# Turning the second unit of each weight-stationary sum, and a smaller bias-row store on another queue

## The chip, the cores and the metric

The kernel runs on one core of one Trainium2 chip. The metric is the time of one execution on the device in microseconds (us), without the host's part. Three runs of the kernel before took 2806.85, 2808.48 and 2808.56 us; the median is 2808.48 us. A profiled execution is one further run, with its own time and its own span (from the first instruction to the last).

## What is computed

A two-layer decoder trunk on one sequence of 256 tokens with model width 2048, all in float32. Layer 0 mixes tokens by retention (8 heads), layer 1 by attention (16 heads of 128) on keys and values that come from the stream after layer 0; each layer then has a squared-ReLU MLP with hidden width 8192 and a gated embedding. Attention adds a bias that depends on the distance between query and key alone:

```python
for i in range(DEPTH):
    if i < N_A_LAYERS:
        h = h + retention(rms_norm(h, ret_norm_g[i]), ret_w_in[i], ret_w_out[i])
    else:
        h = h + moba_attention(rms_norm(h, att_norm_g[j]), att_w_q[j], att_w_o[j],
                               k_blocks, v_blocks, k_means, rel_bias)
    h = h + sq_relu_mlp(rms_norm(h, mlp_norm_g[i]), mlp_w_up[i], mlp_w_down[i])
    h = h + per_layer_embed(h, p[i], ple_norm_g[i], ple_w_up[i], ple_w_gate[i])
return rms_norm(h, final_norm_g)
# inside the attention, with one block of 256 keys:
l_own = jnp.where(dist_own[None] >= 0, l_own + bias_t[:, t5_bucket(dist_own)], NEG_INF)
```

Nearly all the work is the products of the 256 token columns with some 500 MB of weights, each weight used once.

## The kernel before

**Units.** All weights are cut into units of 128 x 1024 numbers (512 KB). Two units come in one load of 1 MB, named `raw` (line 96), issued on the sync engine's queue (SP). `split` (lines 221 and 222) makes two tiles of each unit: `wh`, the weights rounded to the matmul's short format, by a cast on the scalar engine (ACT), and `wl`, what the rounding left, by a subtraction on the vector engine (DVE). Activations are split in the same way into a high part (columns 0 to 255 of a tile) and a low part (columns 256 to 511).

**The sum.** In `mm_a` the weights are the stationary operand. A unit is 8 blocks of 128 rows. First come 8 matmuls with the blocks of `wh` on all 512 columns (line 160; high times high and high times low), then 8 with the blocks of `wl` on the 256 high columns (line 162; low times high). I call them wide and narrow here. `phase_a` runs a weight matrix so: an output tile of 128 rows (`n`) needs `per` units (`u`), 2 or 4 of them, all summed in one PSUM bank. The first `lead` tiles are interleaved (all their units `u` = 0, then all their `u` = 1, and so on), the later ones come one after the other. Phases of this kind have the tile names `qk`, `ret_out`, `up`, `dn`, `gt`, `ak`, `aq` and `att_o`, 788 such units in all. The values and gates of the heads (`v`, `g`, `av`) go through `phase_b` instead, where the activations are stationary and every matmul is wide (lines 212 to 214); `pu` (lines 566 to 568) has narrow ones alone.

**The order of the work** is written out by hand. `run` goes through the units: at unit `i` it issues the load of units `i + 6` and `i + 7` (`load`, for even `i`), the split of unit `i + 3` (`conv`), the matmuls of unit `i`, and then the tasks that `at(i, ...)` hung on that unit, such as the evacuation of a finished bank. Each engine takes its instructions in this order. There are 3 `raw` buffers, 4 of `wh` and 4 of `wl`; a load waits for the subtraction that last read its buffer, a cast waits for the matmuls that last read its `wh`.

**The bias.** `bias_rows` makes 16 rows of 384 numbers, one for each head (`bv`, a small matmul at line 611 and a copy at line 613), while the last units of layer 0's MLP run (`dn`). Line 616 stores them to a scratch tensor `bvec` in HBM, each row 128 times, from SP's queue. In the attention, `table` loads for each group of 4 heads two tiles `T` of 128 x 2 x 256 (line 642): partition p reads copy p of a row, shifted by p, which gives the bias for every query and key.

Of the kernel before, what the change touches and what calls it, by code (L numbers as in the profile page):

```python
# [10 lines left out]
F32 = mybir.dt.float32  # L11
# [6 lines left out]
P = 128  # L18
S = 256
# [5 lines left out]
AH, DH = 16, 128  # L25
GH = 4
# [7 lines left out]
LEAD = 4  # L34
LOOK = 3
WARM = 8
G_RET, G_MLP0, G_PLE0, G_KV, G_ATT, G_MLP1, G_PLE1, G_FIN = range(8)


def order_a(tiles, per, lead):  # L40
    out = [(n, u) for u in range(per) for n in range(lead)]
    return out + [(n, u) for n in range(lead, tiles) for u in range(per)]
# [31 lines left out]
class Core:  # L74
# [70 lines left out]
        return self.wp.tile([P, S], F32, name=name, tag="small", bufs=6)  # L145


    def mm_a(self, ps, wh, wl, rhs, first, last, narrow=False):
        mm = self.nc.tensor.matmul
        cut = [slice(k * P, (k + 1) * P) for k in range(8)]  # L150
        if narrow:
            o = ps[:, :S]
            for k, c in enumerate(cut):
                x = rhs[k]
                mm(o, wh[:, c], x[:, :S], start=first and k == 0, stop=False)
                mm(o, wh[:, c], x[:, S:], start=False, stop=False)
                mm(o, wl[:, c], x[:, :S], start=False, stop=last and k == 7)
            return
        for k, c in enumerate(cut):
            mm(ps, wh[:, c], rhs[k], start=first and k == 0, stop=False)  # L160
        for k, c in enumerate(cut):
            mm(ps[:, S:], wl[:, c], rhs[k][:, :S], start=False, stop=last and k == 7)  # L162

    def phase_a(self, name, src, base, tiles, per, lead, rhs, evac, narrow=(), rush=()):


        banks, ends = {}, {}
        for j, (n, u) in enumerate(order_a(tiles, per, lead)):
            def mm(wh, wl, n=n, u=u):
                if u == 0:  # L170
                    banks[n] = self.bank(f"{name}{n}")
                self.mm_a(banks[n], wh, wl, [rhs(u * 8 + k) for k in range(8)], u == 0, u == per - 1, n in narrow)
            i = self.unit(src, base + j, mm)
            if u == per - 1:
                ends[n] = i
                self.at(i, lambda n=n, i=i: self.steps(i, evac(n, banks.pop(n)), 4 if n in rush else 2 if n == tiles - 1 else 1))
        return ends
# [115 lines left out]
    def start(self):  # L293
# [4 lines left out]
        nc.scalar.activation(warm, self.ones, AF.Silu)  # L298
        self.warm(WARM)
        self.hh = [cp.tile([P, 4, S], F32, name=f"h{q}") for q in range(4)]  # L300
# [297 lines left out]
    def bias_rows(self, i):  # L598
        nc, cp, io = self.nc, self.cp, self.io
        st = {}  # L600

        def load():
            st["rb"] = cp.tile([33, AH], F32, name="relb")
            nc.vector.memset(st["rb"][32:33], NEG)
            nc.sync.dma_start(st["rb"][:32], io["rel_bias"])
            st["oh"] = self.slot("oh", (33, 384))
            nc.sync.dma_start(st["oh"], io["onehot"])

        def rows():
            ps = self.aux("bv")  # L610
            nc.tensor.matmul(ps[:AH, :384], st["rb"], st["oh"], start=True, stop=True)
            st["bv"] = self.slot("bv", (AH, 384))
            nc.vector.tensor_copy(st["bv"], ps[:AH, :384])

        def store():
            nc.sync.dma_start(io["bvec"], st["bv"][:, None, :].to_broadcast([AH, P, 384]))
        self.at(i, load)
        self.at(i + 6, rows)
        self.at(i + 8, store)

    def attention(self):
        nc = self.nc
        mm = nc.tensor.matmul
        first = len(self.units)
# [8 lines left out]
        for g in range(AH // GH):  # L633
            b, st = len(self.units), {}

            def table(st=st, g=g):
                st["T"] = []
                bv = self.io["bvec"]
                for j in range(0, GH, 2):
                    t = self.slot("T", (P, 2, S))  # L640
                    src = bass.AP(tensor=bv.tensor, offset=bv.offset + (g * GH + j) * P * 384 + 127, ap=[[383, P], [P * 384, 2], [1, S]])
                    nc.sync.dma_start(t, src)
                    st["T"] += [t[:, 0], t[:, 1]]
            self.at(b, table)

            def evac_k(n, ps, st=st):
# [91 lines left out]
def program(nc, io):  # L738
    with tile.TileContext(nc) as tc, tc.manual_schedule(), \
            tc.tile_pool(name="const", bufs=1) as cp, tc.tile_pool(name="w", bufs=1) as wp, \  # L740
            tc.tile_pool(name="slots", bufs=59) as sp, \
            tc.tile_pool(name="psum", bufs=1, space=bass.MemoryType.PSUM) as pp, \
            tc.tile_pool(name="dram", bufs=1, space=bass.MemoryType.DRAM) as dp:
        io["bvec"] = dp.tile([AH, P, 384], F32, name="bvec")
        c = Core(nc, tc, (cp, wp, sp, pp), io)
        c.at(-1, c.start)
        c.retention()
        c.x2 = {}
        c.mlp(0, [G_PLE0])
        c.bias_rows(len(c.units) - 30)  # L750
        c.ple(0, [G_KV, G_ATT])
        c.attention()
        c.mlp(1, [G_PLE1])
        c.ple(1, [G_FIN])
        c.end()
        c.run()
# [62 lines left out]
```

## Time and profile before

| What | Value |
|---|---|
| median of three runs | 2808.48 us |
| the profiled execution | 2807.01 us, span 2805.2 us |
| TensorE matmuls (PE) | 2772.9 us busy, 99% of the span, 15482 matmuls |
| TensorE weight loads (PEld) | 2422.7 us, 86% |
| VectorE (DVE) | 1803.8 us, 64% |
| ScalarE (ACT) | 1346.6 us, 48% |
| weights and other DMA | 521.95 MB, mean 186 GB/s |

In the rows that follow, a time at the start of a row is us from the start of the span; the second is the duration of a run of equal instructions, "x8" their count. What stands in square brackets is the time that the engine sat idle before, and what ended it. A matmul's end is modelled and overlaps the next one, so the pace of TensorE is read from the distance between starts. Rows of SP and SPq are issues of transfers; how long a transfer took to land is in the view of DMA issues.

### The profile page before, as it was taken

Reading aid. Unit: us, or ns where it says so; the run is one execution under the profiler, and the core shown is the slowest. Engines: PE = TensorE matmul, PEld = TensorE weight load, DVE = VectorE, ACT = ScalarE, POOL = GpSimd, SP = SyncE. Lnnn points to the kernel's source line nnn. Section 1 sums busy time; section 2 is a strip of 40 time slices with the busy share of each in tenths; the row PEclk is TensorE's granted clock in tenths of the full one; section 3 lists DMA queues with packets and bytes.
Section 4 is the critical chain, followed back from the end, with each engine's and each line's share of the span. In section 5 each row is a group of like instructions: output and inputs, shape, how many; then the busy total and the mean of one; then the engine's idle time right before and its main releaser. Section 6 shows DMA issues by size and latency. Waiting matters only on the chain.

```text
span 2805.2 us, 37950 instructions
## 1 busy us (share of the span) xinstructions
PE 2772.9 (99%) x15482; PEld 2422.7 (86%) x15482; DVE 1803.8 (64%) x2633; ACT 1346.6 (48%) x1901; POOL 0.2 (0%) x4
## 2 busy tenths in 40 slices
PE   9999999999999999999979999999999999999997
PEld 7888888888888888888869888888888888888887
DVE  7766666655566555665647876667665556666666
ACT  5444444444455434444436655555454434544454
POOL 0000000000000000000000000000000000000000
PEclk9999999999999999999989999999999999999999
DMA  6455555555555555555574555455555555555553
GB/s 239 177 183 183 183 183 183 183 195 194 182 188 188 190 189 191 182 194 182 195 189 175 200 179 185 173 180 180 189 186 195 180 194 183 194 191 185 196 180 123
DMA packets 78667, 521.95 MB, mean 186 GB/s; under 512 B 8443, under 2 KB 14492, under 8 KB 16796
## 3 DMA queue, kind: packets, MB, share of 16 engines
q1 hardware_dynamic: 78492, 519.52, 52.6%
q8 instruction: 121, 1.98, 0.3%
q14 instruction: 54, 0.44, 0.1%
HBM read 514.25 MB, written 5.24 MB: 185 GB/s over the span
## 4 chain that ended last, share of the span: by engine, by line
PE 98%; DMA 1%; DVE 0%; ACT 0%; SPq 0%; issue 0%; DVEq 0%; ACTq 0%
PE up L160 17%; PE dn L160 16%; PE up L162 9%; PE dn L162 8%; PE ret_out L160 4%; PE gt L160 4%; PE qk L160 4%; PE ret_out L162 2%; PE ak L160 2%; PE att_o L160 2%; PE aq L160 2%; PE v L212 2%; PE v L213 2%; PE v L214 2%; PE g L212 2%; PE g L214 2%
## 5 line engine op out<-in xcount | busy, mean ns | idle before, releaser
L222 DVE TENSOR_TENSOR wl<-raw,wh 128x1024 fp32r<-128x1024 f32 (+1 forms) x970 | 1179.9, 1221 | 450.3 <-ACT wh L221 433.6
L221 ACT CAST wh<-raw 128x1024 fp32r<-128x1024 f32 (+1 forms) x970 | 1013.9, 1048 | 567.9 <-PE dn L160 234.9
L160 PE MATMUL dn<-a,wh 128*128 128x512 f32 x2048 | 514.8, 393 | 14.5 <-ACT wh L221 14.5
L160 PE MATMUL up<-x,wh 128*128 128x512 f32 x2048 | 513.2, 392 | 0.0
L160 PEld LDWEIGHTS dn<-a,wh 128*128 128x128 f32 x2048 | 369.6, 190 | 81.5 <-ACT wh L221 14.7
L160 PEld LDWEIGHTS up<-x,wh 128*128 128x128 f32 x2048 | 368.3, 189 | 65.9
L162 PEld LDWEIGHTS dn<-a,wl 128*128 128x128 f32 x2048 | 280.2, 191 | 20.1
L162 PEld LDWEIGHTS up<-x,wl 128*128 128x128 f32 x2048 | 279.4, 190 | 20.0
L162 PE MATMUL dn<-a,wl 128*128 128x256 f32 x2048 | 286.4, 283 | 0.0
L162 PE MATMUL up<-x,wl 128*128 128x256 f32 x2048 | 285.5, 282 | 0.0
L226 ACT COPY t<-up 128x256 f32<-128x256 f32 x128 | 47.7, 373 | 329.4 <-PE up L162 329.4
L227 DVE TENSOR_TENSOR t<-t,up 128x256 f32<-128x256 f32 x128 | 53.9, 421 | 215.2 <-ACT t L226 215.1
L160 PE MATMUL ret_out<-ot,wh 128*128 128x512 f32 x512 | 128.3, 392 | 0.0
L160 PE MATMUL gt<-x,wh 128*128 128x512 f32 x480 | 120.6, 393 | 0.0
L160 PE MATMUL qk<-x,wh 128*128 128x512 f32 x448 | 112.6, 393 | 0.0
L160 PEld LDWEIGHTS ret_out<-ot,wh 128*128 128x128 f32 x512 | 92.1, 189 | 16.5
L212 PE MATMUL v<-wh,x 128*128 128x512 f32 x256 | 100.4, 392 | 0.0
L213 PE MATMUL v<-wl,x 128*128 128x512 f32 x256 | 99.7, 389 | 0.0
L212 PE MATMUL g<-wh,x 128*128 128x512 f32 x256 | 99.6, 389 | 0.0
L214 PE MATMUL v<-wh,x 128*128 128x512 f32 x256 | 99.6, 389 | 0.0
L160 PEld LDWEIGHTS gt<-x,wh 128*128 128x128 f32 x480 | 86.3, 189 | 15.4
L213 PE MATMUL g<-wl,x 128*128 128x512 f32 x256 | 99.6, 389 | 0.0
(311 smaller groups left out, 3029.9 us busy)
## 6 DMA issues: line engine op xcount, KB each, us to landing
raw<-mlp_up SPq DMA_DIRECT2D x128, 1024.0 KB, 4.9
raw<-mlp_dn SPq DMA_DIRECT2D x128, 1024.0 KB, 4.9
raw<-ret_in SPq DMA_DIRECT2D x94, 1024.0 KB, 4.9
raw<-att SPq DMA_DIRECT2D x48, 1024.0 KB, 4.9
raw<-ret_out SPq DMA_DIRECT2D x32, 1024.0 KB, 4.9
raw<-ple_gate SPq DMA_DIRECT2D x32, 1024.0 KB, 4.9
raw<-att_o SPq DMA_DIRECT2D x16, 1024.0 KB, 4.9
raw<-ple_up SPq DMA_DIRECT2D x4, 1024.0 KB, 4.9
```

Of the source, the lines that this page charges most:

```text
L160: mm(ps, wh[:, c], rhs[k], start=first and k == 0, stop=False)
L162: mm(ps[:, S:], wl[:, c], rhs[k][:, :S], start=False, stop=last and k == 7)
L212: mm_(banks[t], x[:, a], wh[:, c], start=k == 0, stop=False)
L213: mm_(banks[t], x[:, a], wl[:, c], start=False, stop=False)
L214: mm_(banks[t], x[:, b], wh[:, c], start=False, stop=k == KD - 1)
L221: self.nc.scalar.copy(dst_h, src)
L222: self.nc.vector.tensor_sub(dst_l, src, dst_h.bitcast(F32))
L226: self.nc.scalar.copy(dst, ps[:, :S])
L227: self.nc.vector.tensor_add(dst, dst, ps[:, S:])
```

## The change

There are two edits. In `mm_a`, a unit with odd `u` is "turned": its 8 narrow matmuls with `wl` come first and its 8 wide ones with `wh` last. Units with even `u` and the one tile that goes the `narrow` way (the last of `gt`) stay. The same products are summed in the same bank. Secondly, the scratch tensor has 32 copies of each row instead of 128, its store is issued on ACT's queue, and each `T` tile is loaded by four transfers of 32 partitions, where copy p modulo 32 is read at a shift of its own.

```diff
+BR = 32
-        for k, c in enumerate(cut):
-            mm(ps, wh[:, c], rhs[k], start=first and k == 0, stop=False)
-        for k, c in enumerate(cut):
-            mm(ps[:, S:], wl[:, c], rhs[k][:, :S], start=False, stop=last and k == 7)
+        for low in (True, False) if turned else (False, True):
+            for k, c in enumerate(cut):
+                end = last and k == 7 and low != turned
+                if low:
+                    mm(ps[:, S:], wl[:, c], rhs[k][:, :S], start=False, stop=end)
+                else:
+                    mm(ps, wh[:, c], rhs[k], start=first and k == 0, stop=end)
...
-                self.mm_a(banks[n], wh, wl, [rhs(u * 8 + k) for k in range(8)], u == 0, u == per - 1, n in narrow)
+                self.mm_a(banks[n], wh, wl, [rhs(u * 8 + k) for k in range(8)], u == 0, u == per - 1, n in narrow, u % 2 == 1)
...
-            nc.sync.dma_start(io["bvec"], st["bv"][:, None, :].to_broadcast([AH, P, 384]))
+            nc.scalar.dma_start(io["bvec"], st["bv"][:, None, :].to_broadcast([AH, BR, 384]))
...
-                    src = bass.AP(tensor=bv.tensor, offset=bv.offset + (g * GH + j) * P * 384 + 127, ap=[[383, P], [P * 384, 2], [1, S]])
-                    nc.sync.dma_start(t, src)
+                    for q in range(0, P, BR):
+                        src = bass.AP(tensor=bv.tensor, offset=bv.offset + (g * GH + j) * BR * 384 + 127 - q, ap=[[383, BR], [BR * 384, 2], [1, S]])
+                        nc.sync.dma_start(t[q:q + BR], src)
...
-        io["bvec"] = dp.tile([AH, P, 384], F32, name="bvec")
+        io["bvec"] = dp.tile([AH, BR, 384], F32, name="bvec")
```

The first place is TensorE's order at the seam between the two units of one tile of `up` before the change (`wh` and `wl` with their buffer numbers, `x` is the activation, L160 wide, L162 narrow):

```order
L162 MATMUL up_9_6793<-x_6_5484,wl_6711 128x256
L162 MATMUL up_9_6793<-x_7_5577,wl_6711 128x256
L160 MATMUL up_9_6793<-x_8_5670,wh_6738 128x512
L160 MATMUL up_9_6793<-x_9_5763,wh_6738 128x512
L160 MATMUL up_9_6793<-x_10_5856,wh_6738 128x512
L160 MATMUL up_9_6793<-x_11_5949,wh_6738 128x512
```

And the same seam in the changed kernel, where line 165 is the narrow matmul and line 167 the wide one:

```order
L165 MATMUL up_9_6793<-x_6_5484,wl_6711 128x256
L165 MATMUL up_9_6793<-x_7_5577,wl_6711 128x256
L165 MATMUL up_9_6793<-x_8_5670,wl_6739 128x256
L165 MATMUL up_9_6793<-x_9_5763,wl_6739 128x256
L165 MATMUL up_9_6793<-x_10_5856,wl_6739 128x256
L165 MATMUL up_9_6793<-x_11_5949,wl_6739 128x256
```

Narrow now follows narrow at this seam, and at the end of the turned unit wide follows wide. Over the whole program a wide matmul comes right behind a narrow one 518 times instead of 828, and a narrow one right behind a wide one 516 times instead of 860.

The second place is SP's queue at the end of layer 0's MLP, before the change, with the store of the bias rows among the weight loads:

```order
L96 DMA raw_11992<-mlp_dn 128x2048
L96 DMA raw_12045<-mlp_dn 128x2048
L616 DMA bvec<-bv 2048x1x384
L96 DMA raw_12093<-mlp_dn 128x2048
L96 DMA raw_12142<-mlp_dn 128x2048
L96 DMA raw_12189<-mlp_dn 128x2048
```

In the changed kernel the loads follow each other there (line 97 is the load), and the store, 512 rows of 384 now, stands in ACT's order between the casts of `wh_12047` and `wh_12068`:

```order
L97 DMA raw_11992<-mlp_dn 128x2048
L97 DMA raw_12045<-mlp_dn 128x2048
L97 DMA raw_12093<-mlp_dn 128x2048
L97 DMA raw_12142<-mlp_dn 128x2048
L97 DMA raw_12189<-mlp_dn 128x2048
```

The third place is SP's queue at the first group of the attention, before the change:

```order
L96 DMA raw_13613<-att 128x2048
L96 DMA raw_13686<-att 128x2048
L642 DMA T<-bvec 128x2x256 x2
L96 DMA raw_13755<-att 128x2048
L96 DMA raw_13819<-att 128x2048
```

And in the changed kernel, with the four transfers for each `T` tile:

```order
L97 DMA raw_13613<-att 128x2048
L97 DMA raw_13686<-att 128x2048
L648 DMA T<-bvec 32x2x256 x8
L97 DMA raw_13761<-att 128x2048
L97 DMA raw_13825<-att 128x2048
```

Eight issues stand ahead of the next weight load instead of two, in each of the four groups. The program has 8 counters for the completion of transfers, used in turn, so the eighth of these issues also waits for the landing of the load ahead of the first (`raw_13686`), and the load behind them for the landing of the first `T` transfer.

More of the change, by code (lines that the diff above doesn't have):

```diff
@@ L145, in small, with mm_a @@
         return self.wp.tile([P, S], F32, name=name, tag="small", bufs=6)
-    def mm_a(self, ps, wh, wl, rhs, first, last, narrow=False):
+    def mm_a(self, ps, wh, wl, rhs, first, last, narrow=False, turned=False):
         mm = self.nc.tensor.matmul
```

## The prediction

> **What bounds the kernel now.** I read the page first, then the waits of TensorE (PE), then the time lines at the one long wait, then the pace of TensorE in quiet stretches. From the page, busy time by engine, busy tenths in 40 slices, and the chain of work that ended last:
>
> ```profile
> PE 2772.9 (99%) x15482; PEld 2422.7 (86%) x15482; DVE 1803.8 (64%) x2633; ACT 1346.6 (48%) x1901; POOL 0.2 (0%) x4
> PE   9999999999999999999979999999999999999997
> PE 98%; DMA 1%; DVE 0%; ACT 0%; SPq 0%; issue 0%; DVEq 0%; ACTq 0%
> ```
>
> TensorE is the bound nearly everywhere. One slice dips, the 21st (1402 to 1472 us), and the chain has 1% of DMA. Who waited for whom gives the place; first the longest waits of TensorE, then the one of ScalarE behind it:
>
> ```profile
> PE dn L160 <- ACT wh L221: 14.5, 1, 14.5
> PE st L272 <- DVE acc L251: 2.8, 1, 2.8
> ACT wh L221 <- DMA raw<-mlp_dn: 24.4, 1, 24.4
> ```
>
> So there is one wait of 14.5 us, for a cast that waited 24.4 us for a weight load. All else together is a few us. The time lines of SP, ACT and TensorE around it, and the transfers by issue:
>
> ```profile
> 1404.45 0.69 SPq L616 DMA_DIRECT2D bvec<-bv  x1
> 1408.30 47.03 SPq L96 DMA_DIRECT2D raw<-mlp_dn  x6
> ```
> ```profile
> 1396.64 1.05 ACT L221 CAST wh<-raw 128x1024 fp32r<-128x1024 f32 x1 [1.73 <-PE dn L160]
> ...
> 1408.76 1.05 ACT L221 CAST wh<-raw 128x1024 fp32r<-128x1024 f32 x1 [1.74 <-PE dn L160]
> ...
> 1442.61 1.04 ACT L221 CAST wh<-raw 128x1024 fp32r<-128x1024 f32 x1 [24.41 <-DMA raw<-mlp_dn]
> ```
> ```profile
> 1426.22 2.00 PE L160 MATMUL dn<-a,wh 128*128 128x512 f32 x8
> 1428.07 1.11 PE L162 MATMUL dn<-a,wl 128*128 128x256 f32 x8
> 1443.71 3.78 PE L160 MATMUL dn<-a,wh 128*128 128x512 f32 x8 [14.53 <-ACT wh L221]
> 1447.29 1.91 PE L162 MATMUL dn<-a,wl 128*128 128x256 f32 x8
> 1448.99 2.12 PE L160 MATMUL dn<-a,wh 128*128 128x512 f32 x8
> 1450.95 1.11 PE L162 MATMUL dn<-a,wl 128*128 128x256 f32 x8
> 1451.90 2.00 PE L160 MATMUL dn<-a,wh 128*128 128x512 f32 x8
> ```
> ```profile
> bvec<-bv SPq DMA_DIRECT2D x1, 3072.0 KB, 35.1
> raw<-mlp_dn SPq DMA_DIRECT2D x128, 1024.0 KB, 4.9
> T<-bvec SPq DMA_DIRECT2D x8, 256.0 KB, 5.5
> ```
>
> The store of the bias rows is issued at 1404.45 and lands 35.1 us later, at 1439.6. The load issued behind it at 1408.30 lets its cast begin at 1442.61, although such a load lands in 4.9 us elsewhere. The load stood behind the store in the same queue. When TensorE resumes at 1443.71, its first unit runs at half pace (3.78 and 1.91 where 2.00 and 1.11 are usual).
>
> **The bias store: what goes away.** The pace of a unit comes from a quiet stretch of `up`, first and last rows:
>
> ```profile
> 1112.43 2.00 PE L160 MATMUL up<-x,wh 128*128 128x512 f32 x8
> 1114.27 1.12 PE L162 MATMUL up<-x,wl 128*128 128x256 f32 x8
> 1115.22 2.00 PE L160 MATMUL up<-x,wh 128*128 128x512 f32 x8
> ...
> 1274.44 1.78 PE L160 MATMUL up<-x,wh 128*128 128x512 f32 x7
> ```
>
> From 1112.43 to 1274.44 there are 58 units, so a unit takes 162.01 / 58 = 2.793 us. Between 1426.22 and 1451.90 three units were done in 25.68 us, where 3 x 2.793 = 8.38 would do. The store costs 17.3 us: the wait of 14.5 and 2.8 of slow pace behind it.
>
> Does all of it go? The new store has a quarter of the bytes and of the rows, so I scale its landing to 35.1 / 4 = 8.8 us (an estimate). It is on another queue, but take the bad case that the load still lands only after all of the store: 8.8 + 4.9 = 13.7 us after 1408.30, at 1422.0. TensorE would want the unit at 1426.22 + 2.79 = 1429.0, and in the stalled case it began 1.1 us after the cast's start, so a cast at 1427.9 is early enough: 5.9 us to spare. In the good case, sharing the engines, the load lands sooner still. So the whole 17.3 us go. What is late next at that place is the usual order, cast after matmul, as at 1396.64 and 1408.76 (released by PE).
>
> On ACT the store's issue is new. SP took 0.69 us for four times as many rows; the cast behind it, at 1408.76, had sat idle 1.74 us, so up to 0.69 us there is hidden. It waits for the copy of `bv`, two units earlier in the order, as SP did; behind it are only casts with several us of slack (below). Bounds: 0, or 35.1 us of landing if the quarter-size store is no quicker, which is a rival.
>
> **The `T` loads.** SP issues 8 instead of 2 per group. The first group, SP and then ACT:
>
> ```profile
> 1580.62 5.92 SPq L96 DMA_DIRECT2D raw<-att  x2
> 1586.59 0.94 SPq L642 DMA_DIRECT2D T<-bvec  x2
> 1591.11 5.66 SPq L96 DMA_DIRECT2D raw<-att  x2
> ```
> ```profile
> 1602.28 1.05 ACT L221 CAST wh<-raw 128x1024 fp32r<-128x1024 f32 x1
> ```
>
> Two issues took 0.94, so eight take 3.8 us, to 1590.4; the next load began at 1591.11 anyway. The eighth also waits for the load ahead (issued at the end of the 5.92, about 1586.2) to land, at 1591.1, and the next load for the first `T` transfer, 5.5 us after 1586.6, at 1592.1. That makes the load about 1 us late. It lands at about 1597, and its cast, which came at 1602.28 for reasons of TensorE's, doesn't notice: 5 us to spare. Cost 0; without that cover at most 4 x 1 us.
>
> **The turned units: the pace.** The trace shows what a change between wide and narrow costs. Steady wide matmuls are in a value and gate phase (112 starts from the first to the last row), steady narrow ones in `pu` (86 starts):
>
> ```profile
> 124.83 0.39 PE L213 MATMUL v<-wl,x 128*128 128x512 f32 x1
> ...
> 149.99 0.39 PE L213 MATMUL g<-wl,x 128*128 128x512 f32 x1
> ```
> ```profile
> 1485.78 0.28 PE L566 MATMUL pu<-ph,wh 128*128 128x256 f32 x1
> ...
> 1495.98 0.28 PE L567 MATMUL pu<-pl,wh 128*128 128x256 f32 x1
> ```
>
> A steady wide matmul takes 25.16 / 111 = 0.2267 us, a steady narrow one 10.20 / 85 = 0.1200 us. Eight and eight would be 1.813 + 0.960 = 2.773 us, and a unit takes 2.793: 0.020 us more. By the rows of `up`, the wide block takes 1.84 (1112.43 to 1114.27), 0.027 over steady, and the narrow block 0.953 (the rest of 2.793), 0.007 under. So going from narrow to wide costs about 27 ns and going from wide to narrow gives about 7 back. The turned order has 828 - 518 = 310 fewer of the first and 860 - 516 = 344 fewer of the second: 310 x 0.027 - 344 x 0.007 = 8.4 - 2.4 = 6.0 us saved. With the net 0.020 per pair instead, 6.2 to 6.9. The block's 1.84 is rounded to 0.01, which is worth up to 3 us either way on 310 changes if the narrow side doesn't make up for it. I take 6.0, with 4 to 7 as its bounds.
>
> That it is the change of width, and not the start of a unit with fresh weights, I take from the same rows: the stretch from 124.83 to 149.99 holds some nine unit starts (12 wide matmuls each), all with fresh `wh` and `wl`, and shows no slower pace.
>
> The Trainium skill (TensorE: Matmul & The Clock Gate, section Back-to-back issue gap) has the spacing depend on the width of a matmul alone, which would make any order of the same matmuls worth the same. The rows above, 1.84 for eight wide ones against 8 x 0.2267, speak against it; it is the first rival below.
>
> **The turned units: the waits.** A turned unit reads `wl` at its start, 1.84 us earlier, and frees `wh` at its end, 0.95 us later than now, so the cast three units on may be 0.95 us later. The tightest place outside the stall that I found is in `gt`, where DVE is fullest, DVE and then TensorE:
>
> ```profile
> 1536.00 2.41 DVE L222 TENSOR_TENSOR wl<-raw,wh 128x1024 fp32r<-128x1024 f32 x2
> ```
> ```profile
> 1539.74 1.55 PE L160 MATMUL gt<-x,wh 128*128 128x512 f32 x6
> ```
>
> The first of these two subtractions, done at about 1537.2, makes the `wl` of the unit that begins at 1539.74: 2.5 us ahead of that start. Even with the full 0.95 us lost, 1.6 us are left. So no wait comes in; cost 0. Evacuation starts after a wide matmul instead of a narrow one: it ends 0.39 instead of 0.28 us after its start, but starts 0.11 earlier before the unit's end, so nothing changes there.
>
> **The sum.** The profiled execution took 2807.0 us (span 2805.2, 1.8 around it). 2807.0 - 17.3 - 6.0 = 2783.7 us. The median of the runs is 2808.5, 1.5 above that execution, so I predict 2785.2 us, 0.8% less. A difference of 0.2%, 5.6 us, is about what a measurement of this kernel tells from none.
>
> **The rivals.**
>
> *The order is worth nothing.* The 20 ns belong to something that every unit has, whatever its order, for instance the meeting of its two halves in one bank. For it: `phase_b` sums otherwise, so its flat pace isn't a proof. Against: the excess sits in the wide block behind a narrow one. Then only the store's 17.3 us go: 2808.5 - 17.3 = 2791.2 us. Chance 0.13. This is also what the skill's rule above would give.
>
> *The store still holds up the load.* If the time of the store hangs on something other than its rows (16 source partitions, a write to HBM), or if a store from another queue slows the load just as much, the stall stays in part or whole, and the order alone gains: 2808.5 - 6.0 = 2802.5 us at the worst. It decides from a landing of the load beyond 1427.9, that is 19.6 us after its issue. Against it: three quarters of the rows are gone. Chance 0.06.
>
> *Slower: the `T` loads run one behind the other on SP.* If each of the eight waits for the one before, they take 8 x 5.5 = 44 us and the next load is issued at 1630.6 instead of 1591.1, 39.5 us late. About 5 us of that are hidden by the late cast, and 4 more by the units already split; some 30 us are left in each of four groups, 120 in all: 2785 + 120 = 2905 us. It ends slower than before only if a group loses over 23.3 / 4 = 5.8 us, so if SP is held over 15 us too long. Against it: only the eighth waits for an earlier transfer, and that one lands in 4.9 us. Chance 0.03.
>
> **How the numbers follow.** The forecast has 0.78, with its own range from 2782 to 2789: the bounds of the order's gain (4 to 7), 1 us for runs that scatter, and up to 2 us if a little of the slow pace or of the `T` loads stays. The range takes in the first rival: 2781 to 2792.5. Left out are the second and the third and the tails, under 2 in 10. Faster by over 0.2%: the forecast, the first rival, and half of the second (its worst case gains 6.0, just over the 5.6), 0.94. Same: 0.03. Slower: 0.03.
>
> **What would show it.** In the profile of the changed kernel the dip in the 21st slice is gone, TensorE's longest wait is the 2.8 us at the first statistics, and the cast behind the load of 1408 us waits for PE. Two units of a tile (eight wide, sixteen narrow, eight wide) take about 5.566 us instead of 5.586, so wide blocks come as x16 of about 3.65 us. The store lands in about 9 us. I am wrong if a pair of units still takes 5.586, if TensorE waits for `wl` in `gt`, or if SP's loads behind the `T` transfers come over 5 us later than now.

## The result and the profile after

The changed kernel takes 2784.47 us (median of 4 runs, 2783.93 to 2785.32) against 2808.11 us before (4 runs): a ratio of 0.9918, 95% interval 0.9905 to 0.9930, or 23.6 us less. The forecast was 2785.2. The profiled execution took 2783.96 us with a span of 2782.2.

The page of the changed kernel: busy time, busy tenths in 40 slices, the chain that ended last.

```profile
PE 2763.8 (99%) x15482; PEld 2421.6 (87%) x15482; DVE 1806.4 (65%) x2633; ACT 1343.5 (48%) x1901; POOL 0.2 (0%) x4
PE   9999999999999999999999999999999999999997
PE 99%; DVE 0%; DMA 0%; SPq 0%; ACT 0%; issue 0%; DVEq 0%
```

The dip in the 21st slice is gone and the chain has no DMA worth 1%. What TensorE still waits for, longest first:

```profile
PE st L277 <- DVE acc L256: 2.8, 1, 2.8
PE qk L197 <- ACT wh L226: 2.8, 2, 2.5
```

The second is at the start of the span, with the first loads. Behind the start no wait of TensorE for weights is left in this view, and none for `wl` in `gt`. The place of the old stall in the changed kernel, ACT's time line (the store is issued by ACTq, ACT's own sequencer) and the transfers by issue over the whole run:

```profile
1404.61 1.05 ACT L226 CAST wh<-raw 128x1024 fp32r<-128x1024 f32 x1 [3.02 <-PE dn L167]
1404.91 0.65 ACTq L621 DMA_DIRECT2D bvec<-bv  x1
1406.41 1.05 ACT L226 CAST wh<-raw 128x1024 fp32r<-128x1024 f32 x1 [0.76 <-PE dn L167]
...
1418.44 1.05 ACT L226 CAST wh<-raw 128x1024 fp32r<-128x1024 f32 x1 [1.65 <-PE dn L165]
```
```profile
T<-bvec SPq DMA_DIRECT2D x32, 64.0 KB, 4.5
...
bvec<-bv ACTq DMA_DIRECT2D x1, 768.0 KB, 9.9
```

The store lands in 9.9 us instead of 35.1, and the casts behind it wait for matmuls again, as everywhere else. TensorE's pace shows in its time line through `dn` and `up`, of which these are the first full block, the two behind it and the last one shown:

```profile
1084.16 3.82 PE L167 MATMUL dn<-a,wh 128*128 128x512 f32 x16
1087.82 2.08 PE L165 MATMUL dn<-a,wl 128*128 128x256 f32 x16
1089.73 3.82 PE L167 MATMUL dn<-a,wh 128*128 128x512 f32 x16
...
1256.73 3.59 PE L167 MATMUL up<-x,wh 128*128 128x512 f32 x15
```

Wide and narrow now come in blocks of sixteen. From 1084.16 to 1256.73 there are 62 units: 172.57 / 31 = 5.567 us for a pair of units, where two took 5.586.

### The profile page after: what moved, and what is told of

Read it like the earlier page. It is cut to its first block, busy times and chain, and to the rows that moved or that the text cites. A ratio compares the mean times of both kernels' runs of the same rounds, so it can differ in the third digit from the quotient of the medians.

```text
span 2782.2 us, 37899 instructions
## 1 busy us (share of the span) xinstructions
PE 2763.8 (99%) x15482; PEld 2421.6 (87%) x15482; DVE 1806.4 (65%) x2633; ACT 1343.5 (48%) x1901; POOL 0.2 (0%) x4
## 4 chain that ended last, share of the span: by engine, by line
PE 99%; DVE 0%; DMA 0%; SPq 0%; ACT 0%; issue 0%; DVEq 0%
PE dn L167 17%; PE up L167 17%; PE up L165 9%; PE dn L165 9%; PE ret_out L167 4%; PE gt L167 4%; PE qk L167 4%; PE ret_out L165 2%; PE ak L167 2%; PE aq L167 2%; PE att_o L167 2%; PE v L217 2%; PE g L217 2%; PE v L219 2%; PE g L219 2%; PE v L218 2%
## 5 line engine op out<-in xcount | busy, mean ns | idle before, releaser
L167 PE MATMUL dn<-a,wh 128*128 128x512 f32 x2048 | 493.7, 391 | 0.0
L167 PE MATMUL up<-x,wh 128*128 128x512 f32 x2048 | 490.3, 391 | 0.0
L167 PEld LDWEIGHTS up<-x,wh 128*128 128x128 f32 x2048 | 376.0, 188 | 72.5
L165 PEld LDWEIGHTS dn<-a,wl 128*128 128x128 f32 x2048 | 265.8, 191 | 12.5 <-DVE wl L227 0.6
L165 PEld LDWEIGHTS up<-x,wl 128*128 128x128 f32 x2048 | 263.1, 191 | 10.1
L165 PE MATMUL dn<-a,wl 128*128 128x256 f32 x2048 | 269.7, 283 | 0.0
L165 PE MATMUL up<-x,wl 128*128 128x256 f32 x2048 | 266.9, 283 | 0.0
L167 PEld LDWEIGHTS gt<-x,wh 128*128 128x128 f32 x480 | 87.7, 188 | 16.6
```

Of the source, the lines that this page charges most:

```text
L165: mm(ps[:, S:], wl[:, c], rhs[k][:, :S], start=False, stop=end)
L167: mm(ps, wh[:, c], rhs[k], start=first and k == 0, stop=end)
```

## The experiments

The theory: the store costs 17.3 us because its size holds up the load behind it, and the change of width in the turned units is worth 6.0 us. The rivals: the order is worth nothing; the queue, not the size, is what matters for the store. The first four kernels ran on one chip together with the kernel before (2807.35 us there), the last three on another one, again with the kernel before (2807.43 us); each ratio refers to that.

### The order alone

The changed kernel with the store of before:

```diff
-BR = 32
+BR = 128
...
-            nc.scalar.dma_start(io["bvec"], st["bv"][:, None, :].to_broadcast([AH, BR, 384]))
+            nc.sync.dma_start(io["bvec"], st["bv"][:, None, :].to_broadcast([AH, BR, 384]))
```

> The turned units with the store of before (128 copies, SP's queue, T loads of 128 partitions). My theory: the change of width between matmuls costs 27 ns going to wide and gives 7 ns back going to narrow, so the order alone saves 6.0 us: 2808.1 - 6.0 = 2802.1 us, and TensorE still has one wait of 14 to 15 us behind the store. Rival, the order is worth nothing: 2808 us, with the whole 23.6 us coming from the store.

Measured: 2801.32 us, ratio 0.9978 (0.9969 to 0.9987), 6.0 us below the kernel before. The waits of TensorE, the longest:

```profile
PE dn L167 <- ACT wh L226: 14.6, 1, 14.6
```

The stall is back at full length and the gain of 6.0 us is there beside it. The interval of the ratio leaves out 1, so the rival by which the order is worth nothing falls. It puts the gain between 3.6 and 8.7 us.

### The store alone

The changed kernel with no unit turned:

```diff
-                self.mm_a(banks[n], wh, wl, [rhs(u * 8 + k) for k in range(8)], u == 0, u == per - 1, n in narrow, u % 2 == 1)
+                self.mm_a(banks[n], wh, wl, [rhs(u * 8 + k) for k in range(8)], u == 0, u == per - 1, n in narrow)
```

> The new store and T loads, no unit turned. My theory: 2808.1 - 17.3 = 2790.8 us, no wait of TensorE over 3 us, and units at 2.793 us as before. Rival, the order is worth nothing: 2784.5 us, the same as the changed kernel.

Measured: 2790.49 us, ratio 0.9942 (0.9929 to 0.9954), 16.9 us below the kernel before. TensorE's time line in a quiet stretch, first and last wide block:

```profile
1100.35 2.00 PE L167 MATMUL dn<-a,wh 128*128 128x512 f32 x8
...
1259.57 2.00 PE L167 MATMUL up<-x,wh 128*128 128x512 f32 x8
```

57 units in 159.22 us: 2.793 us each, as before the change. The interval puts the store's part between 12.9 and 19.9 us. The two parts, 6.0 and 16.9, add up to 22.9 of the 23.6 us of both together.

### Twice as many changes of width

As the store alone, but each unit goes in four blocks of four:

```diff
-        for low in (True, False) if turned else (False, True):
-            for k, c in enumerate(cut):
+        for low, part in ((False, 0), (True, 0), (False, 4), (True, 4)):
+            for k, c in list(enumerate(cut))[part:part + 4]:
```

> As store_alone, but each unit goes four blocks wide, four narrow, four wide, four narrow: a wide matmul comes behind a narrow one 1616 times instead of 828, with the same matmuls. If each change costs its full 27 - 7 = 20 ns: 788 x 0.020 = 15.8 us over store_alone, 2806.6 us. If only the first four wide ones behind a change are slow (22 of the 27 ns by their starts in the trace of before), a unit has 2 x 22 - 2 x 8 = 28 ns of excess instead of 20: 788 x 0.008 = 6 us over store_alone, 2797 us. Rival, the excess belongs to the unit and not to the change of width: 0 us over store_alone, 2790.8 us.

Measured: 2800.67 us, ratio 0.9976 (0.9967 to 0.9985), 10.2 us above the store alone: between the two prices that I gave, and far from none. TensorE's time line, the first full block of four and the last one shown, with 97 of them from start to start, and two rows behind the first for the two parts:

```profile
1100.78 1.09 PE L167 MATMUL dn<-a,wh 128*128 128x512 f32 x4
1101.71 0.63 PE L165 MATMUL dn<-a,wl 128*128 128x256 f32 x4
1102.18 1.09 PE L167 MATMUL dn<-a,wh 128*128 128x512 f32 x4
...
1236.90 1.09 PE L167 MATMUL up<-x,wh 128*128 128x512 f32 x4
```

136.12 / 97 = 1.403 us for half a unit, 2.807 for a unit, 13 ns more than 2.793; times 788 units that is 10.5 us. Four wide ones take 0.93 us, 0.023 over 4 x 0.2267, and four narrow ones about 0.473 (the rest of 1.403), 0.007 under 4 x 0.12. So most of the 27 ns lie in the first four wide matmuls behind a narrow one. In this stretch every second wide block begins a unit and the others stand inside one; the two kinds take 0.930 and 0.929 us on average. So the cost goes with the change from narrow to wide, not with the unit.

Two stretches that every kernel here has, with the same order of matmuls, say more on that. In `mm_a` the stationary tile changes (from `wl` to `wh`) whenever the width does, so the tile is a rival. The last tile of `gt` settles it: its matmuls are all narrow and go `wh`, `wh`, `wl`. From the kernel before:

```profile
1581.76 0.28 PE L156 MATMUL gt<-x,wh 128*128 128x256 f32 x1
1581.88 0.28 PE L157 MATMUL gt<-x,wl 128*128 128x256 f32 x1
1582.00 0.28 PE L155 MATMUL gt<-x,wh 128*128 128x256 f32 x1
```

They keep the steady 0.120 us, so going between `wh` and `wl` alone costs nothing. And the price is not the same for every change. In `qk` of the first head, wide and narrow alternate one by one. First and last wide row of a stretch of 34 pairs in the kernel before, then of 37 pairs in the changed kernel:

```profile
19.92 0.40 PE L192 MATMUL qk<-x,wh 128*128 128x512 f32 x1
...
31.93 0.40 PE L192 MATMUL qk<-x,wh 128*128 128x512 f32 x1
```
```profile
19.81 0.39 PE L197 MATMUL qk<-x,wh 128*128 128x512 f32 x1
...
32.64 0.39 PE L197 MATMUL qk<-x,wh 128*128 128x512 f32 x1
```

A pair takes 12.01 / 34 = 0.3532 us and 12.83 / 37 = 0.3468, where steady matmuls would take 0.3467. So a pair of changes costs 7 ns there or nothing, against 16 ns in runs of four and 20 in runs of eight and sixteen. Why the same order has two paces is not shown.

### Turning where tiles are interleaved

```diff
-..., n in narrow, u % 2 == 1)
+..., n in narrow, u % 2 == 1 if n >= lead or lead == 1 else u > 0 and n % 2 == 0)
```

> The changed kernel, with turning in the interleaved tiles by tile number (even tiles of the second and later rounds are turned) so that nearly every seam there joins equal widths. Wide behind narrow 492 times instead of 518, narrow behind wide 495 instead of 516. My theory: 26 x 0.027 - 21 x 0.007 = 0.6 us less than the changed kernel, 2783.9 us, below what the measurement can tell. No theory of mine has it slower; if it is, turning costs something where tiles are interleaved.

Measured: 2783.92 us, ratio 0.9916 (0.9903 to 0.9930). That is the forecast to 0.1 us, but it can't be told from the changed kernel's 2784.47, so it shows neither a gain nor a cost of turning there.

### The queue alone

128 copies, but from ACT's queue:

```diff
-BR = 32
+BR = 128
```

> The changed kernel with 128 copies stored, on ACT's queue, and T loads of 128 partitions as before: only the store's queue differs from order_alone. In the trace of the changed kernel no bytes of the weight load issued at 1406.95 moved while the store ran on its own queue. Theory A, the transfer engines finish the store before they serve the other queue: the wait of 14 to 15 us stays, 2784.5 + 17.3 = 2801.8 us. Theory B, the queues share the engines: the load lands within about 12 us, no wait, 2784.5 us.

Measured: 2786.73 us, ratio 0.9927 (0.9912 to 0.9942). I had read the changed kernel's trace as theory A, and it falls: nearly all of the stall goes with the queue alone. Theory B doesn't hold as it stands either, since the load issued at 1406.55 landed after 19.1 us instead of 12. First the rate of all transfers in the changed kernel, then here, both in 40 slices of 1.1 us from 1402 to 1446 us:

```profile
GB/s 216 410 276 28 102 95 96 103 92 98 126 398 439 402 410 305 372 410 119 0 0 186 410 335 30 74 313 439 127 15 0 179 380 387 242 71 223 447 216 0
```
```profile
GB/s 246 454 179 59 95 102 96 94 105 94 98 102 94 96 103 92 128 334 382 419 421 427 407 431 420 289 145 96 98 98 99 96 99 134 339 410 410 432 425 417
...
raw<-mlp_dn SPq DMA_DIRECT2D x6, 1024.0 KB, 13.3
bvec<-bv ACTq DMA_DIRECT2D x1, 3072.0 KB, 36.0
```

Some 100 GB/s is the store by itself, some 400 means that weight loads move. In the changed kernel the load issued at 1406.95 got nothing for about 7 slices, until the small store was over: so far the store went first there too. With 128 copies the store also goes first, for 13 slices: by 1420.7, 945 of its 2048 rows had moved, which is 59 for each of 16 engines. But then the loads get in, although half the store is still to come, and the store goes on beside them. Transfers by queue (q10 is ACT's, with the store, q1 is SP's, with the loads; number, MB, busy share of 16 engines) from 1406.4 to 1413, where q1 has none, and from 1425 to 1429:

```profile
q10 hardware_dynamic: 419, 0.64, 88.5%
```
```profile
q1 hardware_dynamic: 190, 1.41, 83.3%
q10 hardware_dynamic: 189, 0.29, 19.2%
```

From 1431 to 1439 the store is alone once more, while the load issued at 1430.50 waits. ACT's time line and TensorE's waits in `dn` show what is left of the stall:

```profile
1425.78 1.05 ACT L226 CAST wh<-raw 128x1024 fp32r<-128x1024 f32 x1 [9.38 <-DMA raw<-mlp_dn]
```
```profile
PE dn L167 <- ACT wh L226: 0.7, 2, 0.5
PE dn L165 <- DVE wl L227: 0.6, 1, 0.6
```

ACT sat idle 9.4 us for this load, most of which the units already split cover, and TensorE waits 1.3 us. In order_alone, with the same store on SP's queue, it is 14.6. So a load on the other queue waits for a part of the store, not for all of it. The Trainium skill (DMA: Bandwidth & Descriptors, section Queues, rings and completion order) has an engine go round the queues one packet at a time, of 9 to 17 descriptors typically and 64 at most. As an estimate from the 64, with one row for a descriptor, a load would wait for at most 64 of the 128 rows of an engine; the 59 agree with that limit, and so does the changed kernel, whose 32 rows fit in one such packet; 9 to 17 would not give such waits. That the queues take turns by packets is not shown: from 1420.7 to 1429 both moved in each stretch of 4 us.

### The same store in four pieces

```diff
-            nc.scalar.dma_start(io["bvec"], st["bv"][:, None, :].to_broadcast([AH, BR, 384]))
+            for q in range(0, BR, 32):
+                nc.scalar.dma_start(io["bvec"][:, q:q + 32], st["bv"][:, None, :].to_broadcast([AH, 32, 384]))
```

with `BR = 128` as above.

> As queue_alone, but the store of 128 copies is issued on ACT's queue as four transfers of 32 copies each. Theory A1, the engines serve what was issued first, whatever the queue: the wait stays, 2801.8 us. Theory A2, they change queue between transfers: the weight load gets in after one piece (about 9 us) or two, no wait, 2784.5 us, or up to 2 us more.

Measured: 2788.14 us, ratio 0.9931 (0.9916 to 0.9946). Neither theory: not the full stall, and not free. From the store in one piece it can't be told (2785.67 to 2789.57 us here, 2785.71 to 2787.30 there), and the profiled execution was the slowest of the four. ACT's time line, then TensorE's longest wait:

```profile
1403.78 10.14 ACTq L622 DMA_DIRECT2D bvec<-bv  x4
1414.03 1.05 ACT L226 CAST wh<-raw 128x1024 fp32r<-128x1024 f32 x1 [9.51 <-issue]
...
1440.64 1.04 ACT L226 CAST wh<-raw 128x1024 fp32r<-128x1024 f32 x1 [9.85 <-DMA raw<-mlp_dn]
```
```profile
PE dn L167 <- ACT wh L226: 3.8, 2, 3.2
```

The four issues hold ACT's sequencer for 10.14 us, where the one issue of the same store took 0.65, and the casts behind them on ACT wait 9.51 us for nothing else. TensorE loses 1.2 us by that (0.6 for a cast and 0.6 for a subtraction). Its wait of 3.2 us is for the cast at 1440.64 and so for a load, issued at 1422.5 when about half the store was still to come, which landed after 18.0 us. The rate of transfers, in the same slices:

```profile
GB/s 402 313 81 96 99 94 99 98 95 96 99 98 95 102 95 135 317 380 390 384 401 366 286 250 326 274 182 118 111 128 137 153 171 327 373 424 441 276 82 0
```

It stays near 100 for 13 slices (up to 1418.5), as with the store in one piece, though a piece is over after some 8 us; a piece's end gives the loads no turn. Two of the four pieces had been issued (1403.78 and 1404.17) before the load at 1405.81, so it may be that what is already lined up for the engines goes first; no run shows that.

### The size alone

32 copies, from SP's queue:

```diff
-            nc.scalar.dma_start(io["bvec"], st["bv"][:, None, :].to_broadcast([AH, BR, 384]))
+            nc.sync.dma_start(io["bvec"], st["bv"][:, None, :].to_broadcast([AH, BR, 384]))
```

> The changed kernel with its store of 32 copies on SP's queue. My theory, the size is what counts: the store lands in about 9 us, the load behind it about 14 us after its issue, no wait of TensorE, 2784.5 us. Rival, the other queue is what counts: a wait of TensorE behind the store, up to 2801.8 us.

Measured: 2784.06 us, ratio 0.9918 (0.9902 to 0.9935), the same as the changed kernel. The store by issue, and TensorE's longest wait:

```profile
bvec<-bv SPq DMA_DIRECT2D x1, 768.0 KB, 10.9
```
```profile
PE st L277 <- DVE acc L256: 2.8, 1, 2.8
```

With a quarter of the rows the queue doesn't matter; with all of them another queue saves most of the stall. Either half of the store's edit would have done nearly all of its work: the queue alone 15 of the 17 us, the size alone all of them.

## Why the prediction was right

**The store.** Forecast 17.3 us, measured 16.9 with the store alone. The term was right in its place (the load behind the store) and its size, the 2.8 us of half pace behind the stall included. What the prediction left open is what that half pace is: in the trace of before the granted clock of TensorE (a share of full speed) was 0.50 from 1443.7 to 1449.0 and 1.00 before the stall, and in the changed kernel it stays at 1.00 at this place. So a long wait costs its length and then some; behind the waits of at most 0.6 us in queue_alone the clock stayed at 1.00, and behind the 3.2 us in queue_pieces it was 0.57 over 3.8 us. The store's landing, scaled to 8.8 us, was 9.9. The bad case that I had reckoned with came true: the load waited for all of the store, from another queue too. It landed 11.4 us after its issue, where 13.7 were reckoned and 19.6 would have been too late, so the spare time covered it. By the profile the cast at 1418.44 waited for TensorE, but the load had landed only 0.1 us ahead of it. With the store alone the same cast did wait 1.86 us for the load, and TensorE still had no wait.

**ACT's issue.** I had 0.69 us as its upper bound and a quarter of the rows as a reason for less. It took 0.65: one issue costs the same for 512 rows as for 2048 (0.65 in queue_alone too). It was hidden, since the cast behind it still sat idle 0.76 us.

**The `T` loads.** SP's time line at the first group of the attention in the changed kernel:

```profile
1560.59 5.90 SPq L97 DMA_DIRECT2D raw<-att  x2
1566.54 5.25 SPq L648 DMA_DIRECT2D T<-bvec  x8
1571.88 24.36 SPq L97 DMA_DIRECT2D raw<-att  x5
```

The next load is issued 5.34 us after the first `T` transfer's issue, where it was 4.52 (1591.11 - 1586.59). It is 0.8 us late, against about 1 forecast, and nobody waits for it: no wait of TensorE in the attention is among the longest. The rival by which these loads clog SP falls.

**The order.** Forecast 6.0 us, measured 6.0 with the order alone, and 5.567 us for a pair of units against 5.566 forecast. Sixteen wide ones take 3.654 us on average of the 30 blocks in that stretch, against 3.65. The rival by which spacing hangs on a matmul's width alone is shown wrong for this stream by order_alone and switch_fours: the same matmuls in three orders take three different times. The Trainium skill (TensorE: Matmul & The Clock Gate, section Back-to-back issue gap) gives the gap as a function of a matmul's width, with no term for the matmul before it. The trace doesn't agree, with 1.84 us for eight wide ones behind a narrow one against 8 x 0.2267. That the gain came out at 6.0 is in part luck: the bounds were 4 to 7, and the interval of order_alone is wider than that. What the forecast had loose was how the cost sits in a run. For switch_fours I gave 6 us if the first four hold 22 of the 27 ns and 15.8 if each change costs in full; it is 10.2. Half a unit is 1.403 - 4 x 0.2267 - 4 x 0.12 = 16.6 ns over steady, so a unit has 33 ns of excess where I had put 28: the first four wide ones hold 23 instead of 22, and the narrow side gives back 6 to 7 instead of 8.

**The sum.** 2783.7 us was forecast for the profiled execution and 2783.96 measured; the median was 0.7 us below the forecast. The single parts leave 0.7 us of 23.6 unexplained (22.9 together), which is no more than the runs of one kernel scatter.

## What to carry to other kernels

Before pricing a reorder, compare the steady pace of each kind of matmul with the pace of the mixed blocks: 20 ns for a change of width and back is invisible in any one wait, but 300 of them are 6 us. Take the price from blocks as long as yours, since it was 0 to 7 ns where the widths alternate one by one. A rare transfer of many small rows belongs where no one stands behind it; price it by its landing in the trace, count the slack of the load behind it, and make it smaller first, since a load on another queue still waits for part of it. Cutting the store into pieces gained nothing here, and the issues held the engine's other work for 10 us. A wait that is long enough to lower the granted clock costs more than its length.

## What was not expected of the hardware

- In queue_alone a store on ACT's queue kept a load on SP's queue waiting from 1406.55 to about 1420.7, and then both moved. While both moved the total was about 410 GB/s. The store alone moved about 98 GB/s, beside the loads still some 70 (0.29 MB in 4 us), and it ended after 36.0 us, almost as in the kernel before (35.1): once the loads get in, they cost the store little. Why the store alone is so slow stays open.
- Four issues of 512 rows each held ACT's sequencer for 10.14 us; one issue of 2048 rows took 0.65. The first two of the four took 0.36 and 0.55 us, the other two 4.62 and 4.50. What those two waited for is not shown.
- Behind a narrow matmul the next few wide ones are slower, 23 ns over the first four and 27 over eight, and the first narrow ones behind a wide one a little faster. That this goes with the change of width, and with neither the unit nor the stationary tile, is shown; what in TensorE does it is not.
- Behind the stall of 14.5 us TensorE's granted clock was 0.50 for 5.3 us, which is the half pace of its first matmuls.
